# Unwritten padding tiles that shift five kinds of matmul operands in SBUF against the weight buffers

## The chip, the cores and the metric

The kernel runs on one NeuronCore of a Trainium2 chip. The metric is the device time of one execution in microseconds (us). Three runs of the kernel before took 1157.94, 1159.05 and 1162.96 us; their median is 1159.05 us.

## The reference

The reference is one layer of a streaming encoder on 256 tokens of width 2048, in float32. One input projection of the normalised tokens feeds three branches, and each branch is projected up, gated and summed:

```
h = rms_norm(x, norm_g);  proj = h @ w_in            # 2048 -> 16512 columns
ya = chunked_band_attention(aq, ak, av) * silu(az)   # branch A, 8 heads x 128
yb = rwkv7_time_mix(br, bk, bv, ...) * silu(bz)      # branch B, 16 heads x 64
yc = memory_cross_attention(cq, mk, mv) * silu(cz)   # branch C, 256 memory tokens
merged = sigmoid(ga) * (ya @ w_up_a) + sigmoid(gb) * (yb @ w_up_b) + sigmoid(gc) * (yc @ w_up_c)
return x + merged @ w_o
```

Most of the arithmetic is therefore 256 tokens against weight matrices that are read once from HBM.

## The kernel before, in words

**Weights as a stream.** The host lays all weight matrices out as 185 chunks of 1 MB (128 partitions x 2048 numbers), in the order in which they are used. A chunk lands in one of two `raw` buffers. Each half of it (128 x 1024) is then split into a high part `whi` (ScalarE, L191) and a low part `wlo` = raw - whi (VectorE, L193), both in the format fp32r, with four buffers each.

**Activations in two parts.** The other operand of every projection is split in the same way and kept transposed: `xh`, `xl` for the tokens, `mh`, `ml` for the memory, `yth`, `ytl` for the outputs of branches C and A, `yh`, `yl` for branch B, `gh`, `gl` for the merged branches. These are the five kinds of operands: x, memory, yt, y, g.

**Two shapes of projection.** `proj` (L202 on) streams 512 weight columns through a 128 x 128 block of activations: the weights are the moving operand, the activations the stationary one, which a LDWEIGHTS puts into the array before each matmul. Each half chunk gives 12 such matmuls: four pairs `whi` by the high (L210) and the low part (L211), then four `wlo` by the high part (L215). `proj_cm` (L248 on) turns it round for outputs that are wanted with channels on partitions: a 128 x 128 block of weights is stationary, and 256 token columns of `xh` or `xl` stream through (L259, L260, L262). `proj_last` (L219 on) is the last projection, in parts of 512 and 256 columns (L231, L232, L234).

**Order of the work.** All engines follow the order in which the Python code issues instructions. Small work (norms, attention heads, the recurrence of branch B) is written as generators, and `tick()` steps them on between the half chunks of a projection. No planner or cost table is involved.

**Where the buffers lie.** A tile pool takes bytes of every partition, and the pools of the left side stand one behind the other in the order in which they are opened: constants, weights (`raw`, `whi`, `wlo`), small buffers, x, and then pools that are opened and closed in turn (memory; merged; later y and g). A pool lays its tiles out in the order of their first use. Pools with `side="right"` stand at the other end of the partition. Two padding tiles that nothing writes or reads are in the kernel before: `padw` (24 numbers, ahead of the constants) and `padr` (56 numbers, at the right end).

Of the kernel before, what the change touches and what calls it, by code (L numbers as in the profile page):

```python
# [18 lines left out]
P = 128  # L19
# [71 lines left out]
def build(nc, tc, A, out, dbg=None):  # L91
    dbg = dbg or {}
    ctx = ExitStack()
    with ctx:
        _build(ctx, nc, tc, A, out, dbg)


def _build(ctx, nc, tc, A, out, dbg):
    uid = [0]

    def nm(s):
        uid[0] += 1
        return f"{s}_{uid[0]}"

    def pool(st, name, bufs=1, side=None, space=None):
        kw = {}
        if side:
            kw["side"] = side
        if space is not None:
            kw["space"] = space  # L110
        return st.enter_context(tc.tile_pool(name=name, bufs=bufs, **kw))
# [5 lines left out]
    sm = pool(ctx, "small")  # L117
# [4 lines left out]
    def t(pl, shape, tag, dtype=F32, bufs=1):  # L122
        return pl.tile(shape, dtype, name=nm(tag), tag=tag, bufs=bufs)
# [30 lines left out]
    def advance(tk):  # L154
        try:
            tk[0] = next(tk[1])
        except StopIteration:
            tasks.remove(tk)

    def finish(gen):  # L160
        for tk in list(tasks):
            if tk[1] is gen:
                while tk in tasks:
                    advance(tk)
# [32 lines left out]
    def proj(xh, xl, nk, before=None):  # L197
        acc = [pp.tile([P, 512], F32, name=nm("pp"), tag="pp", bufs=4) for _ in range(2)]
        kt = 0
        while kt < nk:  # L200
            for hi, lo in wchunk():
                if before and kt in before:  # L202
                    finish(before[kt])
                hv = hi.rearrange("p (k n) -> p k n", n=512)
                lv = lo.rearrange("p (k n) -> p k n", n=512)
                last = kt + 2 == nk
                for k2 in range(2):
                    for tt in range(2):
                        sl = slice(tt * P, tt * P + P)
                        T.matmul(acc[tt], xh[:, kt + k2, sl], hv[:, k2], start=(kt + k2 == 0), stop=False)  # L210
                        T.matmul(acc[tt], xl[:, kt + k2, sl], hv[:, k2], start=False, stop=False)  # L211
                for tt in range(2):
                    for k2 in range(2):
                        sl = slice(tt * P, tt * P + P)
                        T.matmul(acc[tt], xh[:, kt + k2, sl], lv[:, k2], start=False, stop=(last and k2 == 1))  # L215
                kt += 2
                tick()
        return acc
# [172 lines left out]
            yield 1  # L391


    xp = ExitStack()
    xpool = pool(xp, "xT")
    xh = t(xpool, [P, 16, S], "xh", F32R)
    xl = t(xpool, [P, 16, S], "xl", F32R)

    padp = pool(ctx, "padr", side="right")
    t(padp, [P, 56], "padr")  # L400
    yc_st = ExitStack()
    ycp = pool(yc_st, "yc", side="right")
    ych = t(ycp, [P, 8, S], "yth", F32R)
# [5 lines left out]
    mv = t(mkp, [P, 2, 1024], "mv")  # L409
    m_st = ExitStack()  # L410
    mp = pool(m_st, "memT")
    mh = t(mp, [P, 16, S], "mh", F32R)
    ml = t(mp, [P, 16, S], "ml", F32R)
    wld = wload()
# [488 lines left out]
    def gate_sig(acc, pl=None, bufs=2):  # L903
        sigs = []
        for tt in range(2):
            sgt = t(pl or mgp, [P, 512], "gsig", bufs=bufs)
            SC.activation(sgt, acc[tt], AF.Sigmoid, scale=rstd_x[:, tt:tt + 1])
            sigs.append(sgt)
        return sigs
# [124 lines left out]
    dump("y_b", zb)  # L1034
    g_st = ExitStack()
    gp = pool(g_st, "gb")
    yh = t(gp, [P, 8, S], "yh", F32R)
    yl = t(gp, [P, 8, S], "yl", F32R)
    yt = spawn(to_T(zb, yh, yl, 0, 8), 1)
    sigs.append(gate_sig(proj(xh, xl, 16), zbp, 8))  # L1040
    finish(yt)
    gh = t(gp, [P, 16, S], "gh", F32R)
    gl = t(gp, [P, 16, S], "gl", F32R)
    for j in range(4):
# [81 lines left out]
```

## Time and profile before

| | |
|---|---|
| median of three runs | 1159.05 us |
| profiled execution | 1165.28 us |
| its span, first to last instruction | 1163.5 us |
| TensorE (PE) busy | 1141.1 us, 98% of the span |
| weight loads of TensorE (PEld) busy | 962.0 us, 83% |
| VectorE (DVE), ScalarE (ACT), GpSimd (POOL) busy | 805.4, 529.6, 167.4 us |
| moved by DMA | 212.75 MB, 183 GB/s on average |

The profiled execution is 6.23 us longer than the median, and 1.78 us of it lie outside the span. A busy interval of a matmul begins when it starts to stream and ends when its results are out, so that neighbouring intervals overlap. What one matmul costs in a row of matmuls is therefore read as the distance from its start to the start of the next one, called the step here; the duration is longer than that.

### The profile page before, as it was taken

How to read it: one execution, taken by the hardware profiler on the slowest of the kernel's cores; microseconds unless marked ns; L12 is line 12 of the kernel's file. 1: busy time of each engine (PE TensorE's matmuls, PEld its weight loads, DVE VectorE, ACT ScalarE, POOL GpSimd, SP SyncE). 2: the span in 40 equal slices, each digit the busy share in tenths (PEclk: the TensorE clock that was granted, in tenths of full speed). 3: DMA queues.
4: the chain of work that ended last, by engine and by line, in shares of the span. 5: the costliest groups of instructions: out<-in, count | busy, mean ns of one | idle time of the engine just before them, and what ended most of it. 6: DMA issues, size and time to landing. Idle time of an engine off the chain costs nothing.

```text
span 1163.5 us, 16874 instructions
## 1 busy us (share of the span) xinstructions
PE 1141.1 (98%) x6610; PEld 962.0 (83%) x6610; DVE 805.4 (69%) x1378; ACT 529.6 (46%) x655; POOL 167.4 (14%) x232
## 2 busy tenths in 40 slices
PE   7999999999999999999999989899999999999998
PEld 6888989889889778988997769787788777888887
DVE  6874566556869657978686778956687956557443
ACT  6754555443642434434453535543453443444332
POOL 0100000034010204010213210213201103300000
PEclk9999999999999999999999999999999999999999
DMA  8765535466474654464644345554355574554663
GB/s 265 252 219 199 187 140 181 153 200 208 150 243 151 199 181 150 149 213 177 199 164 145 109 158 206 171 180 148 129 201 203 178 239 145 190 197 161 230 237 109
DMA packets 36906, 212.75 MB, mean 183 GB/s; under 512 B 5087, under 2 KB 7391, under 8 KB 13275
## 3 DMA queue, kind: packets, MB, share of 16 engines
q1 hardware_dynamic: 29664, 198.59, 49.7%
q0 software_dynamic: 3936, 9.44, 2.9%
q10 hardware_dynamic: 3226, 3.65, 1.0%
q8 instruction: 52, 0.85, 0.3%
q14 instruction: 28, 0.22, 0.1%
HBM read 206.95 MB, written 3.67 MB: 181 GB/s over the span
## 4 chain that ended last, share of the span: by engine, by line
PE 77%; DVE 12%; DMA 5%; issue 2%; ACT 2%; POOL 1%; SPq 0%; ACTq 0%; DVEq 0%; POOLq 0%
PE pp L210 19%; PE pp L211 19%; PE pp L215 18%; DVE wlo L193 4%; PE pp L259 4%; PE pp L262 4%; PE pp L260 4%; DMA raw<-in_wstream_dram 4%; DVE Xu L746 1%; DMA Tu<-scrt 1%; DVE tmu L744 1%; ACT whi L191 1%; PE pp L232 1%; PE pp L234 1%; PE pp L231 1%
## 5 line engine op out<-in xcount | busy, mean ns | idle before, releaser
L193 DVE TENSOR_TENSOR wlo<-raw,whi 128x1024 fp32r<-128x1024 f32 x368 | 456.1, 1251 | 255.2 <-ACT whi L191 253.6
L191 ACT CAST whi<-raw 128x1024 fp32r<-128x1024 f32 x368 | 380.5, 1051 | 536.3 <-PE pp L211 231.0
L210 PE MATMUL pp<-whi,xh 128*128 128x512 f32 x768 | 308.8, 402 | 2.2 <-ACT whi L191 2.1
L211 PE MATMUL pp<-whi,xl 128*128 128x512 f32 x768 | 300.5, 391 | 0.0
L215 PE MATMUL pp<-wlo,xh 128*128 128x512 f32 x768 | 206.6, 391 | 4.6 <-DVE wlo L193 4.6
L215 PEld LDWEIGHTS pp<-wlo,xh 128*128 128x128 f32 x768 | 144.0, 188 | 37.3 <-DVE wlo L193 7.4
L210 PEld LDWEIGHTS pp<-whi,xh 128*128 128x128 f32 x768 | 144.6, 188 | 36.2 <-ACT whi L191 3.5
L211 PEld LDWEIGHTS pp<-whi,xl 128*128 128x128 f32 x768 | 144.8, 189 | 28.8 <-issue 0.5
L259 PE MATMUL pp<-xh,whi 128*128 128x256 f32 x528 | 131.2, 286 | 0.0
L260 PE MATMUL pp<-xl,whi 128*128 128x256 f32 x528 | 129.6, 283 | 0.0
L259 PEld LDWEIGHTS pp<-xh,whi 128*128 128x128 f32 x528 | 101.1, 192 | 1.1 <-issue 0.6
L260 PEld LDWEIGHTS pp<-xl,whi 128*128 128x128 f32 x528 | 101.2, 192 | 0.6 <-issue 0.2
L262 PE MATMUL pp<-xh,wlo 128*128 128x256 f32 x528 | 74.1, 283 | 0.0
L262 PEld LDWEIGHTS pp<-xh,wlo 128*128 128x128 f32 x528 | 68.1, 192 | 0.0
L210 PE MATMUL pp<-whi,mh 128*128 128x512 f32 x128 | 51.6, 403 | 3.3 <-ACT whi L191 2.0
L211 PE MATMUL pp<-whi,ml 128*128 128x512 f32 x128 | 51.0, 398 | 0.2 <-DVE ml L310 0.2
L210 PE MATMUL pp<-whi,yth 128*128 128x512 f32 x128 | 51.0, 398 | 0.0
L211 PE MATMUL pp<-whi,ytl 128*128 128x512 f32 x128 | 49.9, 390 | 0.0
L744 DVE TENSOR_TENSOR tmu<-Tu,Xu 128x112 f32<-128x112 f32 (+29 forms) x124 | 32.7, 263 | 15.2 <-DMA Tu<-scrt 12.1
L210 PE MATMUL pp<-whi,gh 128*128 128x512 f32 x96 | 37.4, 390 | 0.0
L211 PE MATMUL pp<-whi,gl 128*128 128x512 f32 x96 | 37.4, 389 | 0.0
L746 DVE TENSOR_TENSOR Xu<-Xu,tmu 128x112 f32<-128x112 f32 (+29 forms) x124 | 32.7, 264 | 3.0
(258 smaller groups left out, 1349.4 us busy)
## 6 DMA issues: line engine op xcount, KB each, us to landing
raw<-in_wstream_dram SPq DMA_DIRECT2D x184, 1024.0 KB, 5.0
xraw<-in_xT_dram SPq DMA_DIRECT2D x8, 256.0 KB, 5.4
Tu<-scrt POOLq DMA_DIRECT2D x4, 512.0 KB, 4.9
xr<-in_x_dram POOLq DMA_DIRECT2D x8, 256.0 KB, 5.2
xraw<-in_memT_dram SPq DMA_DIRECT2D x7, 256.0 KB, 5.0
out_dram<-xr POOLq DMA_DIRECT2D x6, 256.0 KB, 3.4
bias<-in_rel_dram POOLq DMA_DIRECT2D x4, 256.0 KB, 3.7
tmpA<-in_bc_dram ACTq DMA_DIRECT2D x8, 128.0 KB, 4.2
```

Of the source, the lines that this page charges most:

```text
L191: SC.copy(hi, sl)
L193: V.tensor_tensor(out=lo, in0=sl, in1=hi.bitcast(F32), op=ALU.subtract)
L210: T.matmul(acc[tt], xh[:, kt + k2, sl], hv[:, k2], start=(kt + k2 == 0), stop=False)
L211: T.matmul(acc[tt], xl[:, kt + k2, sl], hv[:, k2], start=False, stop=False)
L215: T.matmul(acc[tt], xh[:, kt + k2, sl], lv[:, k2], start=False, stop=(last and k2 == 1))
L231: T.matmul(acc, xh[:, kt + k2, sl], hv[:, k2, cs], start=(kt + k2 == 0), stop=False)
L232: T.matmul(acc, xl[:, kt + k2, sl], hv[:, k2, cs], start=False, stop=False)
L259: T.matmul(acc, hv[:, k2], xh[:, kt + k2, :], start=(kt + k2 == 0), stop=False)
L260: T.matmul(acc, hv[:, k2], xl[:, kt + k2, :], start=False, stop=False)
L262: T.matmul(acc, lv[:, k2], xh[:, kt + k2, :], start=False, stop=(kt + k2 == 15))
L744: V.tensor_tensor(out=tv, in0=Tu[:, s, s + 1:32].unsqueeze(2).to_broadcast([P, n, m]), in1=X[:, s:s + 1, 0:m].to_broadcast([P, n, m]), op= ...
L746: V.tensor_tensor(out=X[:, s + 1:32, 0:m], in0=X[:, s + 1:32, 0:m], in1=tv, op=ALU.add)
```

## The change

Four padding tiles are added and one is made smaller. No instruction is added, removed or moved: both programs have the same instructions on every engine, in the same order, with the same shapes and the same semaphore waits. What differs is where tiles lie in the partition.

```
+    t(sm, [P, 32], "padx")            # small buffers, ahead of x: 128 bytes
     xp = ExitStack()
     xpool = pool(xp, "xT")
 ...
-    t(padp, [P, 56], "padr")          # right end: 224 bytes
+    t(padp, [P, 32], "padr")          # 128 bytes
 ...
     mp = pool(m_st, "memT")
+    t(mp, [P, 8], "padm")             # ahead of memory: 32 bytes more
     mh = t(mp, [P, 16, S], "mh", F32R)
 ...
     gp = pool(g_st, "gb")
+    t(gp, [P, 24], "pady")            # ahead of y: 96 bytes more
     yh = t(gp, [P, 8, S], "yh", F32R)
 ...
+    t(gp, [P, 16], "padg")            # ahead of g: another 64 bytes
     gh = t(gp, [P, 16, S], "gh", F32R)
```

The comments with byte counts are added here. `padx` becomes the first tile of the small buffers, since it is used first, and moves everything behind it. The first byte of each operand in a partition, and its distance from the weight buffers modulo 256 bytes (all `raw`, `whi` and `wlo` buffers begin at multiples of 512 in both kernels):

| operand | before | after | distance before | distance after |
|---|---|---|---|---|
| `whi` (first buffer) | 26112 | 26112 | 0 | 0 |
| x: `xh` | 59392 | 59520 | 0 | 128 |
| memory: `mh` | 92160 | 92320 | 0 | 160 |
| yt: `yth` | 212736 | 212832 | 0 | 96 |
| y: `yh` | 150528 | 150752 | 0 | 224 |
| g: `gh` | 166912 | 167200 | 0 | 32 |

Modulo 512, `yth` stands at 256 in the kernel before and the other four at 0. The low parts lie a multiple of 512 behind the high ones. The blocks that one matmul takes out of these tiles begin at multiples of 512 bytes within a tile. All other tiles of the left side move by 128 bytes (those of the memory pool by 160), all other tiles of the right side by 96; `raw`, `whi`, `wlo` and the constants stay.

## Rows read from the trace of the kernel before

**Rows 1.** The page: span, TensorE, granted clock, chain that ended last.
```profile
span 1163.5 us, 16874 instructions
PE 1141.1 (98%) x6610; PEld 962.0 (83%) x6610; DVE 805.4 (69%) x1378; ACT 529.6 (46%) x655; POOL 167.4 (14%) x232
...
PEclk9999999999999999999999999999999999999999
...
PE 77%; DVE 12%; DMA 5%; issue 2%; ACT 2%; POOL 1%; SPq 0%; ACTq 0%; DVEq 0%; POOLq 0%
```

**Rows 2.** What TensorE waited for: us in all, times, longest.
```profile
PE pp L215 <- DVE wlo L193: 4.6, 4, 2.8
PE pp L210 <- ACT whi L191: 4.1, 2, 2.1
```

**Rows 3.** Instructions that touch `wlo`: count, ns min/median/max, first and last start.
```profile
L215 PEld LDWEIGHTS pp<-wlo,xh x768: 186/188/334, 104.9 to 1024.6; 128*128 128x128 f32 x192
L215 PE MATMUL pp<-wlo,xh x768: 388/389/632, 105.2 to 1024.8; 128*128 128x512 f32 x192
L262 PEld LDWEIGHTS pp<-xh,wlo x528: 192/192/192, 126.9 to 720.7; 128*128 128x128 f32 x176
L262 PE MATMUL pp<-xh,wlo x528: 279/283/283, 127.0 to 720.8; 128*128 128x256 f32 x176
...
L215 PE MATMUL pp<-wlo,mh x128: 388/389/593, 9.7 to 102.6; 128*128 128x512 f32 x128
...
L215 PE MATMUL pp<-wlo,yth x128: 388/389/389, 308.4 to 900.8; 128*128 128x512 f32 x128
...
L215 PE MATMUL pp<-wlo,gh x96: 389/389/393, 1073.1 to 1137.2; 128*128 128x512 f32 x96
...
L215 PE MATMUL pp<-wlo,yh x64: 389/389/393, 1026.9 to 1071.0; 128*128 128x512 f32 x64
...
L234 PE MATMUL pp<-wlo,gh x48: 279/283/393, 1138.3 to 1159.8; 128*128 128x256 f32 x32, 128*128 128x512 f32 x16
```

**Rows 4.** Timeline of TensorE around 542 us: start us, length us, operands, count.
```profile
540.76 0.39 PE L210 MATMUL pp<-whi,xh 128*128 128x512 f32 x1
...
542.57 1.07 PE L215 MATMUL pp<-wlo,xh 128*128 128x512 f32 x4
543.48 0.39 PE L210 MATMUL pp<-whi,xh 128*128 128x512 f32 x1
```

**Rows 5.** Timeline of TensorE around 594 us, 256 columns.
```profile
593.05 0.28 PE L259 MATMUL pp<-xh,whi 128*128 128x256 f32 x1
...
594.49 1.12 PE L262 MATMUL pp<-xh,wlo 128*128 128x256 f32 x8
```

**Rows 6.** Timeline of TensorE around 1140 us, 512 and 256 columns in turn.
```profile
1138.35 0.61 PE L234 MATMUL pp<-wlo,gh 128*128 128x512 f32 x2
1138.80 0.28 PE L231 MATMUL pp<-whi,gh 128*128 128x256 f32 x1
1138.91 0.28 PE L232 MATMUL pp<-whi,gl 128*128 128x256 f32 x1
1139.03 0.28 PE L231 MATMUL pp<-whi,gh 128*128 128x256 f32 x1
...
1140.23 0.40 PE L231 MATMUL pp<-whi,gh 128*128 128x512 f32 x1
1140.46 0.40 PE L232 MATMUL pp<-whi,gl 128*128 128x512 f32 x1
1140.70 0.39 PE L231 MATMUL pp<-whi,gh 128*128 128x512 f32 x1
1140.93 0.40 PE L232 MATMUL pp<-whi,gl 128*128 128x512 f32 x1
1141.16 0.62 PE L234 MATMUL pp<-wlo,gh 128*128 128x512 f32 x2
1141.62 0.28 PE L231 MATMUL pp<-whi,gh 128*128 128x256 f32 x1
```

**Rows 7.** Longest pieces of the chain that ended last: start us, length us.
```profile
149.16 3.46 PE ps L496 x16
...
342.49 6.37 DMA Tu<-scrt
```

**Rows 8.** DMA issues: count, KB each, median us from issue to landing.
```profile
raw<-in_wstream_dram SPq DMA_DIRECT2D x184, 1024.0 KB, 5.0
...
Tu<-scrt POOLq DMA_DIRECT2D x4, 512.0 KB, 4.9
```

More of the change, by code (lines that the diff above doesn't have):

```diff
@@ L391, in to_T @@
             yield 1
+    t(sm, [P, 32], "padx")
     xp = ExitStack()
@@ L399, in _build @@
     padp = pool(ctx, "padr", side="right")
-    t(padp, [P, 56], "padr")
+    t(padp, [P, 32], "padr")
     yc_st = ExitStack()
@@ L411, in _build @@
     mp = pool(m_st, "memT")
+    t(mp, [P, 8], "padm")
     mh = t(mp, [P, 16, S], "mh", F32R)
@@ L1036, in _build @@
     gp = pool(g_st, "gb")
+    t(gp, [P, 24], "pady")
     yh = t(gp, [P, 8, S], "yh", F32R)
@@ L1041, in _build @@
     finish(yt)
+    t(gp, [P, 16], "padg")
     gh = t(gp, [P, 16, S], "gh", F32R)
```

## The prediction, made before the changed kernel was run

> **What bounds the kernel now.** I read the page first, then the waits of TensorE, then the timeline of its matmuls. On the page TensorE is busy for 98% of the span, at a granted clock of 9 tenths or more in every slice, and 77% of the chain that ended last is its work [rows 1]. The waits confirm it: its longest sums are 4.6 us for `wlo` and 4.1 us for `whi` [rows 2]. A change that alters no instruction can therefore pay or cost only through the step from one matmul to the next, and the step is what the timeline is read for.
>
> How many steps there are follows from the rows on `wlo`. Each `wlo` matmul has two `whi` ones beside it, so the matmuls of 512 columns are 3 x (768 + 128 + 128 + 96 + 64 + 16) = 3,600, of which 3 x 768 = 2,304 take x, and those of 256 columns are 3 x (528 + 32) = 1,680, of which 1,584 stream x [rows 3].
>
> What a step takes: from 540.76 to 543.48 us there are 12 matmuls of 512 columns, 2.72 us, that is 226.7 ns each [rows 4]. At 2.4 GHz 512 columns are 213.3 ns, so each step carries 13.3 ns, or 32 clocks, on top. From 593.05 to 594.49 us there are 12 matmuls of 256 columns, 1.44 us, or 120 ns each, again 13.3 ns over the 106.7 ns of the columns [rows 5]. Steps alone make 3,600 x 0.2267 + 1,680 x 0.120 = 816 + 202 = 1,018 us of the 1,163.5.
>
> **What the change can touch.** While one matmul streams its columns, the LDWEIGHTS for the next one reads the other operand. These are the two reads whose distance changes: 0 before, and 128 (x), 160 (memory), 96 (yt), 224 (y), 32 (g) afterwards. The question is whether the step depends on that distance.
>
> What speaks for it is that the step is not one fixed number. In the last projection, where parts of 512 and 256 columns alternate, the six steps from 1140.23 to 1141.62 us take 231.7 ns on average, single ones 230 and 240 ns by the rows, while the same matmuls elsewhere take 226.7 [rows 4, 6]. These have the same tiles, the same addresses and the same clock. Only the moment differs at which the weight load starts against the stream, since the matmuls before had 256 columns. The weight loads beside 512 columns take 188 ns and those beside 256 columns 192 ns [rows 3]. So the two reads do disturb each other, by some nanoseconds.
>
> What speaks against it: distances of whole multiples of 256 bytes make no difference at all. `yth` stands 256 bytes off modulo 512, the other four at 0, and the median duration is 389 ns for all five [rows 3]. And the 13.3 ns do not look like a collision with the weight load. The first 256-column matmul after 512-column ones takes from 1138.80 to 1138.91 us, the next from 1138.91 to 1139.03 [rows 6]. At this resolution that is 110 and 120 ns, so the first is nearer to the columns plus half of 13.3 ns (113.3 ns). Then the extra time goes with the columns streamed, one clock in 16, and not with the number of weight loads, which is one per matmul at either width. An extra that belongs to the stream itself doesn't change with where the weights for the next matmul lie.
>
> The Trainium skill ("SBUF — State Buffer", section "SBUF: two separate sides") says that the engine ports of TensorE wait on nobody, and "TensorE: Matmul & The Clock Gate" (section "Step-by-step: what each phase is for") that loading the next weights takes no read bandwidth from the running matmul. By that rule no address could matter and the sum would be nothing; the rows just shown, 231.7 against 226.7 ns, disagree with it by 5 ns, so I do not take it as certain.
>
> **The sum.** Five terms, against the profiled execution of 1,165.28 us.
> 1. 3,600 steps of 512 columns: I take 0. From above, if every one went to the disturbed 231.7 ns, 3,600 x 5.0 = 18.0 us; if every one went to the 240 ns of the longest single one as the rows print it, 3,600 x 13.3 = 48 us. From below, if the whole 13.3 ns went, -48 us. I take 0 because 226.7 is both the commonest step and, with x, memory, yt, y and g alike, the one to which the stream settles by itself.
> 2. 1,680 steps of 256 columns: I take 0. From below 113.3 instead of 120 ns, 1,680 x 6.7 = 11.3 us less; from above the same 6.7 ns more, 11.3 us.
> 3. The split of the weights (L191, L193) reads and writes only `raw`, `whi` and `wlo`, none of which moves: 0.
> 4. Other VectorE, ScalarE and GpSimd work moves with its tiles by 96 or 128 bytes, mostly both operands alike: 0. The stream of TensorE hides it: TensorE is idle for only 1163.5 - 1141.1 = 22.4 us of the span [rows 1], so these engines are late rarely, and 10% on what they are late by would be 2 us without cover.
> 5. Small DMAs into tiles that moved. The one on the chain is `Tu<-scrt`, 6.37 us at one place, four of them of 4.9 us [rows 7, 8]. I take 0; 10% either way would be 4 x 0.5 = 2 us. The 184 weight loads land in `raw`, which stays.
>
> The padding itself costs nothing: no instruction writes it. The sum is 0, and the profiled execution would stay at 1,165.28 us, 6.23 us above the median of the runs shown; for the median that is 1159, and I say 1160.
>
> **The rivals.**
> *Slower: the stream does not settle.* Mechanism: with x 128 bytes off, a weight load and the stream beside it keep meeting in the bad relation that is seen at 1140 us, instead of falling back to 226.7 ns after a few steps. Place: the 2,304 steps with x, and perhaps all 3,600. Price: 2,304 x 5.0 = 11.5 us for x, 18.0 us for all. TensorE waits little, so I count nine tenths, 10 to 16 us: 1170 to 1176, taken as 1173, with a tail to 1190 if the steps are nearer to the longest ones. It decides from 229.2 ns on for the x steps (5.8 us / 2,304 = 2.5 ns). For: the 5 ns are in the trace at unchanged addresses. Against: multiples of 256 bytes do nothing, and every kind of operand settles within a few matmuls.
>
> *Faster: the narrow matmuls settle better.* At 120 ns the 256-column steps are 6.7 ns above the single 113 ns step, with a weight load 4 ns longer than beside wide matmuls [rows 3, 6]. If 128 bytes of distance take that relation away, 1,584 x 6.7 = 10.6 us go, some 10 on the path: 1149. Against: a weight load may simply need 120 ns, and then nothing moves.
>
> *Much faster: the 13.3 ns are a collision after all.* A plain fp32 matmul of 256 columns takes 3.46 us / 16 = 216 ns, which is two passes of 106.7 ns and only 3 ns over [rows 7], so the array itself does not need the 13.3 ns; both reads are slower there. If another distance took it away, 3,600 x 11 + 1,680 x 11 = 58 us would go from TensorE, of which I count three quarters, since the weights then come too slowly at times (1 MB lands in 5.0 us [rows 8], a chunk of 24 steps would last 24 x 0.216 = 5.2 us): 1160 - 44 = 1116. Against: the 113 ns step, and no sign of it at 256 bytes.
> The Trainium skill ("TensorE: Matmul & The Clock Gate", section "Wait — 56ns, not 53.3ns?") gives 215.7 ns as the step of warm matmuls of 512 columns. By it the 226.7 ns of this trace hold 11 ns that are not the matmul's own, and this rival would have more to it; no fp32r row here shows a step of that length.
>
> That the change does not do what it says is excluded: the addresses in the table of the change are those of the built programs, and every wait is the same, so no buffer is reused earlier or later than before.
>
> **How the numbers follow.** No effect 46%, slower 31%, narrow steps faster 15%, much faster 8%. A measurement of this kernel tells 0.5%, 5.8 us, from no change: the first case lies within it, 1156 to 1164, and the others outside. So faster 0.23, same 0.46, slower 0.31. The range goes from 1140 to 1184: it leaves out the much faster case and the tail of the slower one, some 14% together, and holds the bounds of terms 2, 4 and 5.
>
> **What would show it.** In the changed kernel the twelve steps of a half chunk with x should again take 2.72 us, and those of 256 columns 1.44 us; memory, yt, y and g should show 389 ns, as x does. The argument is wrong if the steps differ between the five operands: each has its own distance now, so an effect of distance must show as five different steps. The slower rival shows as x steps of over 229 ns and weight loads of over 188 ns; the narrow rival as L262 weight loads under 192 ns.

## The result, and the profile after

The changed kernel is slower: 1175.42 us (median of four runs, 1174.4 to 1175.7) beside 1160.3 us for the kernel before, a ratio of 1.0109 with a 95% interval of 1.0085 to 1.0133. The likeliest case of the prediction, no effect, did not come true; the slower rival did, within 3 us of its 1173. The range, 1140 to 1184, holds the result only because it was drawn wide enough to take in most of that rival; the sum had none of the loss.

The page of the changed kernel has the same instructions and the same clock, and TensorE fills more of the chain that ended last: 87% instead of 77%, at the cost of VectorE (12% to 6%) and DMA (5% to 3%) [rows 1]. Not all of these ten points belong to the change: a kernel below that takes as long as the one before (x at 240) shows 81%.

```profile
span 1173.9 us, 16874 instructions
PE 1155.2 (98%) x6610; PEld 960.7 (82%) x6610; DVE 805.0 (69%) x1378; ACT 529.7 (45%) x655; POOL 167.7 (14%) x232
...
PEclk9999999999999999999999999999999999999999
...
PE 87%; DVE 6%; DMA 3%; ACT 1%; issue 1%; POOL 1%; SPq 0%; DVEq 0%; ACTq 0%; POOLq 0%
```

The rows on `wlo` (count, ns min/median/max, first and last start) answer to [rows 3]: there the median of the wide matmuls, of 512 columns, was 389 ns for all five operands. Now it is 393, 394, 397, 395 and 395, a different one for nearly each.

```profile
L215 PEld LDWEIGHTS pp<-wlo,xh x768: 186/188/329, 105.6 to 1031.9; 128*128 128x128 f32 x192
L215 PE MATMUL pp<-wlo,xh x768: 388/393/578, 105.8 to 1032.1; 128*128 128x512 f32 x192
L262 PEld LDWEIGHTS pp<-xh,wlo x528: 187/189/193, 128.1 to 723.3; 128*128 128x128 f32 x176
L262 PE MATMUL pp<-xh,wlo x528: 277/282/290, 128.2 to 723.4; 128*128 128x256 f32 x176
...
L215 PE MATMUL pp<-wlo,mh x128: 389/394/399, 9.8 to 103.3; 128*128 128x512 f32 x128
...
L215 PE MATMUL pp<-wlo,yth x128: 391/397/400, 311.5 to 906.9; 128*128 128x512 f32 x128
...
L215 PE MATMUL pp<-wlo,gh x96: 393/395/396, 1081.6 to 1147.6; 128*128 128x512 f32 x96
...
L215 PE MATMUL pp<-wlo,yh x64: 393/395/402, 1034.2 to 1079.5; 128*128 128x512 f32 x64
```

The timeline of TensorE in the changed kernel (start us, length us, operands, count) shows the step itself. Twelve matmuls with x took 2.72 us [rows 4]; now they take 2.80 us from 542.05 and 2.78 us from 544.85, so 233 and 232 ns each.

```profile
542.05 0.39 PE L210 MATMUL pp<-whi,xh 128*128 128x512 f32 x1
...
543.91 1.10 PE L215 MATMUL pp<-wlo,xh 128*128 128x512 f32 x4
544.85 0.39 PE L210 MATMUL pp<-whi,xh 128*128 128x512 f32 x1
...
547.63 0.40 PE L210 MATMUL pp<-whi,xh 128*128 128x512 f32 x1
```

For the sum I took all steps (start to start) of the two profiled executions apart, by operand. A step counts as short below 300 ns for wide matmuls; the longer ones hold a wait or other small work.

| wide matmuls with | count | mean short step before, ns | after, ns | count x difference, us |
|---|---|---|---|---|
| x | 2,304 | 227.8 | 232.5 | 10.8 |
| memory | 384 | 227.4 | 233.4 | 2.3 |
| yt | 384 | 227.3 | 234.2 | 2.6 |
| y | 192 | 226.9 | 233.3 | 1.2 |
| g | 336 | 227.2 | 233.1 | 2.0 |

That is 18.9 us. The narrow matmuls of 256 columns give back 0.9 us (x: 119.9 to 119.4 ns). The two spans differ by only 10.4 us. A part of this lies in the waits: what the long steps hold above a short one is 26.7 us before and 22.7 us after with x, 6.9 and 5.3 us with memory. That the slower steps shortened these waits is not shown, since they vary from one execution to the next: with x at distance 0 in both, they are 26.4 us in the first experiment below and 22.1 us in "Four more". The median moved by more, 15.1 us; the profiled execution of before was itself 5 us above the median in this comparison.

### The profile page after: what moved, and what is told of

Same layout as the page of the kernel before. It is cut to its first block, busy times and chain, and to the rows that moved or that the text cites. A ratio compares the mean times of both kernels' runs of the same rounds, so it can differ in the third digit from the quotient of the medians.

```text
span 1173.9 us, 16874 instructions
## 1 busy us (share of the span) xinstructions
PE 1155.2 (98%) x6610; PEld 960.7 (82%) x6610; DVE 805.0 (69%) x1378; ACT 529.7 (45%) x655; POOL 167.7 (14%) x232
## 4 chain that ended last, share of the span: by engine, by line
PE 87%; DVE 6%; DMA 3%; ACT 1%; issue 1%; POOL 1%; SPq 0%; DVEq 0%; ACTq 0%; POOLq 0%
PE pp L210 22%; PE pp L211 21%; PE pp L215 21%; PE pp L259 5%; PE pp L260 5%; PE pp L262 5%; DVE wlo L193 2%; DMA raw<-in_wstream_dram 2%; PE pp L234 1%; PE pp L232 1%; PE pp L231 1%; PE ps L533 1%; PE ps L498 1%; PE ps L710 1%; PE ps L834 1%
## 5 line engine op out<-in xcount | busy, mean ns | idle before, releaser
L193 DVE TENSOR_TENSOR wlo<-raw,whi 128x1024 fp32r<-128x1024 f32 x368 | 455.4, 1248 | 264.7 <-ACT whi L191 256.2
L191 ACT CAST whi<-raw 128x1024 fp32r<-128x1024 f32 x368 | 380.8, 1049 | 546.7 <-PE pp L211 271.7
L210 PE MATMUL pp<-whi,xh 128*128 128x512 f32 x768 | 312.2, 407 | 1.7 <-ACT whi L191 1.7
L211 PE MATMUL pp<-whi,xl 128*128 128x512 f32 x768 | 303.6, 395 | 0.0
L215 PE MATMUL pp<-wlo,xh 128*128 128x512 f32 x768 | 210.2, 395 | 3.7 <-DVE wlo L193 3.7
L215 PEld LDWEIGHTS pp<-wlo,xh 128*128 128x128 f32 x768 | 144.5, 189 | 39.2 <-DVE wlo L193 5.4
L210 PEld LDWEIGHTS pp<-whi,xh 128*128 128x128 f32 x768 | 144.9, 189 | 38.2 <-ACT whi L191 3.2
L211 PEld LDWEIGHTS pp<-whi,xl 128*128 128x128 f32 x768 | 145.1, 189 | 31.1 <-issue 0.5
L210 PE MATMUL pp<-whi,mh 128*128 128x512 f32 x128 | 51.4, 402 | 3.6 <-ACT whi L191 1.9
L210 PE MATMUL pp<-whi,yth 128*128 128x512 f32 x128 | 51.8, 404 | 0.0
L211 PE MATMUL pp<-whi,ml 128*128 128x512 f32 x128 | 50.6, 395 | 0.2 <-DVE ml L310 0.2
L211 PE MATMUL pp<-whi,ytl 128*128 128x512 f32 x128 | 50.7, 396 | 0.0
L746 DVE TENSOR_TENSOR tmu<-Tu,Xu 128x112 f32<-128x112 f32 (+29 forms) x124 | 32.6, 263 | 13.3 <-DMA Tu<-scrt 10.2
L210 PE MATMUL pp<-whi,gh 128*128 128x512 f32 x96 | 38.1, 397 | 0.0
L211 PE MATMUL pp<-whi,gl 128*128 128x512 f32 x96 | 37.9, 395 | 0.0
L215 PE MATMUL pp<-wlo,yth 128*128 128x512 f32 x128 | 35.2, 396 | 0.0
```

Of the source, the lines that this page charges most:

```text
L191: SC.copy(hi, sl)
L193: V.tensor_tensor(out=lo, in0=sl, in1=hi.bitcast(F32), op=ALU.subtract)
L746: V.tensor_tensor(out=tv, in0=Tu[:, s, s + 1:32].unsqueeze(2).to_broadcast([P, n, m]), in1=X[:, s:s + 1, 0:m].to_broadcast([P, n, m]), op= ...
```

## The experiments

In all of them "distance" is that of the activations from the weight buffers, modulo 256 bytes. Step means are of short steps as above. A line with dots marks left-out code.

**Only the weights' side moves.**

```
-    t(cp, [P, 24], "padw")
+    t(cp, [P, 56], "padw")
```

> The kernel before with padw 128 bytes larger: the weight buffers and everything behind them on the left side (x, memory, y, g) move together by 128 bytes, yt stays. Distances from the weights: x, memory, y, g 0, yt 128. Distance theory (the step depends on how far the two tiles that TensorE reads at the same time lie apart, modulo 256 bytes): x, memory, y and g step at 226.7 to 228 ns as before, and only the 384 matmuls with yt, which itself has not moved, rise to 232 to 234 ns, some 2.5 us in all; time within 0.4% of before, about 1162. Address theory (what counts is whether the activations, or the weights, begin at a multiple of 256 by themselves): x, memory, y and g, and the weights, are off by 128, so 3,200 steps rise to 232 to 234 ns and yt may stay; time about 1173. Theory that the layout at large matters (other engines or DMAs into moved tiles): steps unchanged, time near 1170.

Measured: ratio 1.0021 (1.0007 to 1.0036). Steps with x 227.8, memory 227.3, y 226.9, g 227.2 ns, with yt 232.5 ns. The rows on `wlo` of this kernel (columns as above):

```profile
L215 PE MATMUL pp<-wlo,xh x768: 387/389/565, 103.5 to 1023.7; 128*128 128x512 f32 x192
...
L215 PE MATMUL pp<-wlo,yth x128: 388/393/404, 306.9 to 900.2; 128*128 128x512 f32 x128
```

All tiles of the left side lie at new addresses, and only the tile that has not moved, yt, became slow. So it is the distance between the two tiles, not the address of either, and the address theory falls. That other engines' tiles moved cost nothing to be seen.

**x alone.**

```
+    t(sm, [P, 32], "padx")          # x at 128 (comments added here)
 ...
     xl = t(xpool, [P, 16, S], "xl", F32R)
+    t(xpool, [P, 32], "padx2")      # what follows x at 256
```

> The kernel before with x alone at distance 128; a second padding tile behind x brings memory, y and g to 256 bytes, that is distance 0 again, and yt stays at 0. Distance theory: the x steps of 512 columns rise to 232.5 ns as in the changed kernel (2,304 x 4.7 = 11 us of steps, less some 5 us of waits that shrink), all others stay at 226.7 to 227.5; time 1167 to 1170, about two thirds of the loss. If the loss came from the other four kinds or from other engines' tiles: 1160. If any shift of a tile cost something, memory, y and g at 256 bytes would rise to 233 as well and the time be 1175.

Measured: ratio 1.0051 (1.0034 to 1.0068), 1166.67 beside 1160.88 us. Steps with x 232.4 ns, with memory, y and g, which have moved by 256 bytes, 227.6, 227.0 and 227.2. In its rows on `wlo` x stands at 393 and g at 389:

```profile
L215 PE MATMUL pp<-wlo,xh x768: 388/393/628, 103.5 to 1026.7; 128*128 128x512 f32 x192
...
L215 PE MATMUL pp<-wlo,gh x96: 389/389/393, 1074.9 to 1139.0; 128*128 128x512 f32 x96
```

The distance theory holds; x is about half of the loss in time, a little less than the two thirds that I expected.

**All but x.** Against the changed kernel:

```
-    t(sm, [P, 32], "padx")
 ...
-    t(mp, [P, 8], "padm")
+    t(mp, [P, 40], "padm")
 ...
-    t(gp, [P, 24], "pady")
+    t(gp, [P, 56], "pady")
```

> The changed kernel with x put back to distance 0 and memory, yt, y, g left at 160, 96, 224, 32. Distance theory: x steps return to 227.8 ns, the other four stay at 233 to 234; of the loss of 1.09% the part that e2_x_only does not have remains, about 0.6%, 1166 to 1168. If the parts do not add (each loss absorbed by waits on the other engines): 0.3% or less.

Measured: ratio 1.0044 (1.0026 to 1.0063). Steps with x are back at 227.7 ns; memory, yt, y and g stand at 233.4, 234.1, 233.2 and 233.1, as in the changed kernel. That is a little under the 0.6% expected. The two parts add, 0.51% and 0.44% beside 1.09% with intervals of 0.2% each, so within these intervals no part of the loss needs another cause.

**Other distances, and a mixed one.** Against the kernel before (`gl` as `gh`):

```
     xh = t(xpool, [P, 16, S], "xh", F32R)
+    t(xpool, [P, 32], "padxl")
     xl = t(xpool, [P, 16, S], "xl", F32R)
+    t(xpool, [P, 32], "padx2")
 ...
-    t(padp, [P, 56], "padr")
+    t(padp, [P, 48], "padr")
 ...
+    t(mp, [P, 16], "padm")
 ...
+    t(gp, [P, 48], "pady")
 ...
-    gh = t(gp, [P, 16, S], "gh", F32R)
+    t(gp, [P, 16], "padg")
+    gh = t(gp, [P, 16 * S + 64], "gh", F32R)[:, 4:4 + 16 * S].rearrange("p (k s) -> p k s", s=S)
```

> The kernel before with distances not tried yet, read by the steps of each kind: x high part at 0 and low part at 128, memory at 64, yt at 32 (the value that g had in the changed kernel), y at 192, g at 16 bytes. Collision theory (the load of the NEXT matmul's stationary block disturbs the stream of the matmul that runs): with x, steps from L210 to L211 run beside a load of the low part and rise to about 232, while L215 steps, whose next load is of the high part, stay at 226.7. Own-operand theory (a matmul is slow by its own stationary block): L211 steps rise, L210 stay. Theory that the value of the distance counts and not the kind of operand: yt at 32 alternates 232 and 235 as g did, mean 233.3. For 64, 192 and 16 nothing is known: 226.7 to 234; a value under 226.7 would point to a faster kernel than before. Time 1163 to 1172.

Measured: one run of 1175.45 us, 3 us above the range expected. The steps: memory at 64 bytes 233.4 ns, yt at 32 233.2 ns (g at 32 had 233.1), y at 192 229.1 ns, g at 16 227.3 ns. So at 32 bytes the value counts and not the kind. With x, here are two half chunks in the timeline of TensorE in this kernel:

```profile
1005.38 0.40 PE L210 MATMUL pp<-whi,xh 128*128 128x512 f32 x1
...
1007.24 1.09 PE L215 MATMUL pp<-wlo,xh 128*128 128x512 f32 x4
1008.17 0.40 PE L210 MATMUL pp<-whi,xh 128*128 128x512 f32 x1
...
1032.14 0.40 PE L210 MATMUL pp<-whi,xh 128*128 128x512 f32 x1
...
1034.01 1.07 PE L215 MATMUL pp<-wlo,xh 128*128 128x512 f32 x4
1034.91 0.39 PE L210 MATMUL pp<-whi,yh 128*128 128x512 f32 x1
```

In the second, the eight matmuls of L210 and L211, where loads at distance 0 (`xh`) and 128 (`xl`) alternate, take 1.87 us or 233.8 ns each. The four of L215, whose own and next blocks are all `xh`, take 0.90 us, 226 or 227 ns each: the step is back at once. In the first the eight take 1.86 us, but the four 0.93 us: 231, 236, 228 and 232 ns in the trace. Of the 109 half chunks with x that hold no long step, the four take 226 to 228 ns on the mean in 59 and 231 to 232 ns in 46. Neither of the two theories stands as I wrote it: L210 steps (own block at 0, next load at 128) are slow, and L211 steps (own at 128, next load at 0) are too, 231 to 235 ns on the mean at each of the eight places. On the mean, steps were fast only where both are at 0, and there only in about half of the half chunks. Since a disturbed row of matmuls can stay slow for some steps, this run does not tell which of the two loads disturbs it.

**Shorter loads.** On top of "x alone", L215 takes 64 columns for every first block of a pair:

```
+                        c = 64 if k2 == 0 else P
-                        sl = slice(tt * P, tt * P + P)
-                        T.matmul(acc[tt], xh[:, kt + k2, sl], lv[:, k2], ...)
+                        sl = slice(tt * P, tt * P + c)
+                        T.matmul(acc[tt][:c], xh[:, kt + k2, sl], lv[:, k2], ...)
```

> The kernel e2_x_only (x alone at distance 128), but every first matmul of a pair in L215 has a stationary block of 64 columns instead of 128, so its weight load reads half as many bytes. It leaves out the low-part correction for half of the tokens of every second block of rows. In the twelve matmuls of a half chunk the short loads belong to the 9th and the 11th, and they run beside the 8th and the 10th. Collision theory (the load of the next block slows the running stream): with x the 8th and 10th steps fall from 232 to 227 to 230 ns while the 9th and 11th stay at 231 to 233. Own-operand theory (a matmul is slowed by its own block): the 9th and 11th fall, the 8th and 10th stay. If the load has nothing to do with it: all twelve stay at 232.4. With y and g, at distance 0, all steps stay at 226.7 in every theory.

Measured: one run of 1171.16 us. For x the twelve steps do not separate (231.8 ns on the mean; the 8th to 11th 229.8, 229.5, 229.7, 230.9), so the question it was made for stays open. What no theory had said is that the kinds at distance 0 changed as well. With g, eight steps stay at 227 and the four of L215 become 236, 228, 233 and 230 ns in every half chunk. In the timeline of this kernel (where L215 has become L216) the four begin at 1101.29 and the next at 1102.21, 0.92 us as the rows print it and 927 ns as the sum of the four, where four steps of 226.7 ns make 907:

```profile
1101.29 1.09 PE L216 MATMUL pp<-wlo,gh 128*64 128x512 f32 x4
1102.21 0.39 PE L210 MATMUL pp<-whi,gh 128*128 128x512 f32 x1
```

They stream 512 columns as ever; the block of every first one was made half as wide, and with it its load and its output, and the matmuls got longer. Which of the two did it, the shorter load or the narrower output, the run doesn't tell. These are almost the numbers of the last projection of the kernel before, after narrow matmuls (233, 236, 228, 233, 230 ns, the steps of [rows 6]), and of the slow half chunks of the run above. So I read 226.7 ns as the step of a regular train in which load and stream keep one relation: in these three places, what upset the train cost some nanoseconds a step over the next matmuls.

**Below 32 bytes.** Views that begin 4, 2, 6 and 1 numbers into larger tiles for x, memory, y and g, as `gh` above; for x and yt:

```
-    xh = t(xpool, [P, 16, S], "xh", F32R)
-    xl = t(xpool, [P, 16, S], "xl", F32R)
+    xx = t(xpool, [P, 32 * S + 64], "xx", F32R)
+    xh = xx[:, 4:4 + 16 * S].rearrange("p (k s) -> p k s", s=S)
+    xl = xx[:, 4 + 16 * S:4 + 32 * S].rearrange("p (k s) -> p k s", s=S)
 ...
-    t(padp, [P, 56], "padr")
+    t(padp, [P, 8], "padr")
```

> The kernel before with distances below 32 bytes, by views that begin some numbers into a larger tile: x at 16 bytes, memory at 8, y at 24, g at 4, and yt at 192. In e3_scan g at 16 bytes stayed at 227.3 ns for 512 columns and its 256-column steps fell from 119.5 to 118.3. If only the position within 32 or 64 bytes is free: x, memory, y and g all stay at 227 to 228 for 512 columns. If 16 was one lucky value: 4, 8 or 24 bytes rise to 230 to 234. yt at 192 should show what y showed there, steps of 226, 229 and 232 in turn, mean 229.1. The 1,584 steps of 256 columns with x fall by about 1.2 ns, 2 us; time 1158 to 1161 against 1160, or 1157 if nothing else changes: a kernel that could be as fast as before or a little faster.

Measured: ratio 1.0055 (1.0034 to 1.0076). Memory at 8 bytes 230.7, y at 24 231.0, g at 4 232.4, yt at 192 229.3 ns (y there 229.1). x at 16 bytes came to 231.3 ns, although g at 16 had 227.3. That mean belongs to no half chunk: the twelve matmuls of one take either 2.80 us or 2.72 us, with the same tiles at the same addresses, as the timeline of this kernel shows (`xx` is the tile that holds `xh` and `xl`).

```profile
121.24 0.40 PE L210 MATMUL pp<-whi,xx 128*128 128x512 f32 x1
...
124.04 0.40 PE L210 MATMUL pp<-whi,xx 128*128 128x512 f32 x1
...
537.58 0.39 PE L210 MATMUL pp<-whi,xx 128*128 128x512 f32 x1
...
540.30 0.39 PE L210 MATMUL pp<-whi,xx 128*128 128x512 f32 x1
```

Of 110 half chunks with x without a long step, 32 have 227 or 228 ns as their mean step and 78 have 233 or 234, none a value between. So at that distance the train has two lasting states, and what decides between them is not shown. The hope for a faster kernel falls; the narrow steps fell as expected, to 118.1 ns, but the wide ones with x cost three times as much.

**Four more, and the one that looked free.** Views again, 60, 63 and 52 numbers into their tiles for memory, y and g; x as before:

```
-    t(padp, [P, 56], "padr")
+    t(padp, [P, 40], "padr")
 ...
-    mh = t(mp, [P, 16, S], "mh", F32R)
+    mh = t(mp, [P, 16 * S + 64], "mh", F32R)[:, 60:60 + 16 * S].rearrange("p (k s) -> p k s", s=S)
```

> The kernel before with four more distances, x left at 0: memory at 240, yt at 64 (the value that memory had in e3_scan), y at 252, g at 208 bytes. If a distance near a multiple of 256 from below is as good as 0: memory and y stay near 227. If only 0 settles: 229 to 235 for all four, yt near 233.4 as memory at 64. A step under 226.7 would be a kernel faster than before; I expect none. x stays at 227.8 ns. Time 1162 to 1168.

Measured: one run of 1163.17 us beside 1157.63. Memory 228.2, yt 233.3, y 231.1, g 231.9 ns; the 231.1 of y at 252 is again a mixture, of half chunks at 227 and at 233 ns. At 240 the wide step is nearly free, so x was put there, with the rest at 0:

```
-    xh = t(xpool, [P, 16, S], "xh", F32R)
-    xl = t(xpool, [P, 16, S], "xl", F32R)
+    xx = t(xpool, [P, 32 * S + 64], "xx", F32R)
+    xh = xx[:, 60:60 + 16 * S].rearrange("p (k s) -> p k s", s=S)
+    xl = xx[:, 60 + 16 * S:60 + 32 * S].rearrange("p (k s) -> p k s", s=S)
```

> The kernel before with x alone at distance 240, the only value besides 0 at which the wide steps stayed low (memory at 240: 228.2 ns); all other kinds at 0. If the value decides: wide x steps at 228 to 229 ns, up to 3 us of steps more than before; the 1,584 narrow steps, in which the load stands 16 bytes off the stream seen the other way round, fall from 119.9 to about 118.3 as g did at 16 bytes, 2.5 us less. Net between -2 and +1 us, 1157 to 1161 beside 1159: no kernel that beats before by a measurable amount. If the wide steps with x settle worse than those with memory did (as x at 16 bytes did against g at 16): 231 ns, 7 us more steps, 1163.

Measured: ratio 0.9999 (0.9981 to 1.0017). Wide steps with x 228.0 ns, narrow ones 117.2 ns instead of 119.9. By steps alone that is 1,584 x 2.7 - 2,304 x 0.2 = 3.8 us less, about 0.3%, and none of it shows in the time. No distance tried beats the kernel before.

All wide steps by distance, in ns:

| distance | mean step |
|---|---|
| 0 and 256 | 226.9 to 227.8, all five kinds |
| 4, 8, 24 | 232.4 (g), 230.7 (memory), 231.0 (y) |
| 16 | 227.3 (g), 231.3 (x) |
| 32, 64, 96 | 233.1 (g) and 233.2 (yt), 233.4 (memory) and 233.3 (yt), 234.2 (yt) |
| 128, 160 | 232.5 (x, yt), 233.4 (memory) |
| 192, 208, 224 | 229.1 (y) and 229.3 (yt), 231.9 (g), 233.3 (y) |
| 240, 252 | 228.2 (memory) and 228.0 (x), 231.1 (y) |

The 231.3 at 16 and the 231.1 at 252 bytes mix the two states, near 227 and 233 ns.

## Why the prediction was right or wrong

**What bounds the kernel** was read rightly: no instruction changed, and the steps of TensorE grew by more than the median did, 18.0 us in sum against 15.1 us.

**Term 1, the wide steps, is the step that failed.** I took 0 and it was 18.9 us, just over the 18.0 us that I had as the bound for every step at the disturbed 231.7 ns. The reason that I gave for 0 was that 226.7 is where the stream "settles by itself". The trace showed that only at distance 0: modulo 256 bytes, the kernel before has no other. The second reason, that `yth` at 256 bytes did not differ [rows 3], is true and stays true in "x alone", but it says nothing of distances below 256. I extended it to them. The sign that I had named for being wrong, steps that differ between the five operands, is what the trace of the changed kernel showed.

**The argument from the narrow matmul** (110 against 120 ns) was used too widely. That the 13.3 ns belong to the stream is not contradicted: no distance gave a lasting step under 226.7 ns, and the much faster rival is ruled out at the 14 distances tried. But it answers whether the step can fall, not whether it can rise.

**The plain fp32 matmul** behind the much faster rival was misread, though nothing in the result hangs on it. The 16 records of L496 in [rows 7] are 8 matmuls of the code, two records each, so such a matmul took 432 ns and not 216. Nor do the rows say that "both reads are slower there": the weight loads beside these records take 187 to 192 ns in the trace, as those of [rows 3] do.

**Term 2, the narrow steps:** 0 predicted, -0.9 us measured for the changed kernel. At other distances they do move, to 117.2 ns with x at 240 and 116.8 with g at 208, so narrow steps do depend on distance, by some 3 of the 6.7 ns that this rival counted on, and 128 bytes is not the distance for it. The weight load beside them shortened as that rival asked, from 192 to 189 ns.

**Terms 3 to 5 held.** The split of the weights takes what it took, 1248 ns in L193 and 1049 ns in L191, where it took 1251 and 1051 ns before, and the DMAs into moved tiles did not get slower. Here are two rows of the page before and four of that of the changed kernel (mean ns after the comma in the rows of L193 and L191, then the idle time before them and what ended it; KB each and median us to landing in the others; [rows 8] has 5.0 and 4.9 us):

```profile
L193 DVE TENSOR_TENSOR wlo<-raw,whi 128x1024 fp32r<-128x1024 f32 x368 | 456.1, 1251 | 255.2 <-ACT whi L191 253.6
L191 ACT CAST whi<-raw 128x1024 fp32r<-128x1024 f32 x368 | 380.5, 1051 | 536.3 <-PE pp L211 231.0
```

```profile
L193 DVE TENSOR_TENSOR wlo<-raw,whi 128x1024 fp32r<-128x1024 f32 x368 | 455.4, 1248 | 264.7 <-ACT whi L191 256.2
L191 ACT CAST whi<-raw 128x1024 fp32r<-128x1024 f32 x368 | 380.8, 1049 | 546.7 <-PE pp L211 271.7
...
raw<-in_wstream_dram SPq DMA_DIRECT2D x184, 1024.0 KB, 5.0
...
Tu<-scrt POOLq DMA_DIRECT2D x4, 512.0 KB, 4.4
```

**The slower rival** was right in place and price: all 3,600 steps rather than those of x alone, 4.7 ns with x and 6 to 7 ns with the others where I had 5.0, against its point of decision of 229.2 ns for x the measured 232.5. Its mechanism, steps that stay in a bad relation of load and stream, fits the cycles in the trace, but its weight loads of over 188 ns did not show; their median stayed at 188. Of 18.0 us of steps 15.1 us reached the median (9.9 to 15.4 by the interval), a little less than its nine tenths, and 10.4 us the two profiled spans. Where the rest went is not shown. That ScalarE idles longer until L211 lets it go on, 271.7 us against 231.0 (rows of L191 above), fits an engine that waits more for a slower TensorE. Its chance of 31% was too small: the 231.7 ns of [rows 6] were direct evidence of two reads that disturb each other, and I set against it only evidence at one residue of the address.

**The page's rule** that loading the next weights takes nothing from the running matmul (the Trainium skill, "TensorE: Matmul & The Clock Gate", section "Step-by-step: what each phase is for") does not hold for these matmuls as the prediction took it, that no address could matter: by the first experiment the step depends on the distance of the two tiles, 227.3 against 232.5 ns with yt.

**What stays open** is how the two reads share the memory. The runs show that the step depends on the distance modulo 256, and that at distance 0 a change of width or a narrower block makes it grow too. Every matmul here has a load beside its stream, so that the load is needed for it is argued and not shown. The runs don't show which of the two reads is held up, nor why 240 bytes cost little, nor what decides at 16 and 252 bytes between the state near 227 and that near 233 ns.

## What to carry to other kernels

In fp32r matmuls like these, with a weight load beside every stream, the placement of the two operands is a parameter of the kernel: here up to 3% of a wide step and 1.1% of the time, with the same instructions. Keep the tiles that TensorE streams and those that it loads at one residue modulo 256 bytes, and look again after any new small buffer ahead of them. To read such an effect, don't use busy time: take the steps from start to start, by operand, and see whether the operands differ.

## What was not expected of the hardware

- The step repeats in short cycles that belong to the distance, as with x at 128 bytes in the changed kernel (241, 233, 230, 232, 228, 230, 233 ns; in other stretches 229, 238) or g at 32 (235, 232), and not as noise.
- Stationary blocks half as wide made the wide matmuls around them longer, 236, 228, 233 and 230 ns instead of 226.7, with both tiles at distance 0.
- At 16 bytes the same tiles at the same addresses give lasting steps of 227 or of 233 ns in one execution.
- The same instructions have narrow steps with x of 117.2 to 119.9 ns by placement alone.
